# Strassen's seven half products for five projections of two column groups, in a hybrid SSM and pooling layer

## The chip, the cores and the metric

The kernel runs on one core of a Trainium2 chip. Its engines are PE (matrix products), DVE (vector operations), ACT (activations and copies), POOL (vector operations, and here the issue of some DMAs) and SP (issue of DMAs); each works through its own instructions in order, and semaphores tie them together. The metric is device microseconds of one launch; the median of three runs is given.

## What is computed

One inference step of a layer with two branches. 2064 prompt tokens (16 meta tokens ahead of 2048) and 8 x 8 sample tokens of 1024 features are normalised and projected six ways; an SSM branch and a causal pooling branch follow, each gated, and all is merged and added to the input. In float32:

```python
xn = rmsnorm(h, norm_gain)
proj = xn @ w_in                       # u_s, z_s, u_p, z_p and two gates, 1024 columns each
gates = jax.nn.sigmoid(proj[..., o4:] + b_gate)
y_s, new_re, new_im = ssm_branch(u_s, s0_re, s0_im, ...)   # scan, gelu, y * sigmoid(y @ w_glu + b_glu)
y_p, new_buf = pool_branch(u_p, buf, pos0, pool_mix, pool_scale)  # windows 2, 4, 8, 16, then a 256x256 mix each
a = y_s * jax.nn.silu(z_s)
b = y_p * jax.nn.silu(z_p)
merged = g_s * (a @ w_branch_ssm) + g_p * (b @ w_branch_pool)
return h + merged @ w_out, new_re, new_im, new_buf
```

The final norm and the new states are outputs as well.

## The kernel before

Features lie on the 128 partitions (eight blocks of 128), tokens along the free dimension, in four groups of columns (`GROUPS`): 544, 536, 536 and 512 wide. Group 3, the last one, holds the sample tokens too.

**Products.** Each operand is split into a high and a low part in the fp32r format, and a product is three matmuls: high by high, weight high by input low, weight low by input high (`mm3`, lines 126 to 128). `proj` makes one output block: eight input blocks, two halves of the columns in groups 0 to 2 (268 columns each in groups 1 and 2), one bank of 512 columns in group 3. That is one *unit*: 48 matmuls, or 24 in group 3. Its result lies in a PSUM tile `acc` of two banks; there are three such tiles, and a new unit takes the next one once the reader of its former contents is done.

**The list of units** is written out by hand for each stage: `up`, `zp` and `mix` of the pooling branch in the order of the string `ORDER`, then `gate` and `brp`, `zs`, `glu`, `gate` and `brs`, `out`. The main loop (line 1288 on) runs it. At unit i it issues the cast of the weights of unit i+2 to their high part (`w_high`, POOL), the posts of unit i-1 (what reads its PSUM: ACT or DVE, and what follows), events tied to the unit, the unit's matmuls with pieces of the SSM between them, then the weight low of unit i+2 (`w_low`, DVE, line 202) and loads of the weights of units i+3 to i+5 (`w_load`, SP, three buffers `raw`). A post therefore stands on its engine behind all that earlier units issued there.

**Pooling.** `up`'s post copies its block to `E` (ACT, line 797), POOL adds the two columns of history (line 800), DVE forms the running sums over 2, 4, 8 or 16 tokens (lines 813 to 823); `po_split` splits the result for `mix`, whose post (line 878) multiplies the gate in `H` by the mix in PSUM. One unit `mix` serves two blocks.

**The SSM** runs in two rounds of 32 pairs, 37 *ticks* each, spread over units of other work: round 0 over units 39 to 72, round 1 over units 76 to 212, none in the pooling stages (`spread`). Each tick issues small matmuls into the tiles `sx` and `sy`, DVE scans, ACT copies and POOL products; the result of a pair goes out from the one buffer `sY` by a DMA to `ys` (line 579).

```python
def st_out(g, q):
    y = stile("sY", 1, g.kn)
    A.activation(y, pr.pop(q)["py"], AF.Copy)
    SY.dma_start(chans(g, ys_d, q), y)
```

## Time and profile before

| | us |
|---|---|
| median of three runs | 2161.5 (2160.64 to 2164.21) |
| profiled run | 2158.2 |
| span of its trace | 2156.4 |
| busy PE, DVE, POOL, ACT | 2084.8, 1395.2, 931.2, 686.5 |

The trace is of one execution; its times count from the start of the span. The granted clock is TensorE's, 1.00 for its full speed, the mean of the span is 0.99. "DMA share" is the mean busy share of the core's 16 DMA engines. In a timeline a number in brackets is how long the engine stood idle before the instruction, and on whom it waited. Stages, in us: the SSM's first round to unit 72 ends at about 578; groups 2 and 3 begin their pooling stages at about 1284 and 1735.

### The profile page before, as it was taken

What the parts mean: (1) busy time and instruction counts of PE and PEld (TensorE: products, weight loads), DVE (VectorE), ACT (ScalarE), POOL (GpSimd) and SP (SyncE); (2) the same over time, 40 slices, a digit from 0 to 9 for tenths busy, and PEclk for the clock granted to TensorE, in tenths of its full rate; (3) what the DMA queues carried; (4) which work ended last, traced back from release to release, by engine and by line L of the source; (5) the groups of instructions that cost most, each with busy time, mean ns of one, the idle gap of its engine ahead of it and who ended that gap; (6) DMA issues with size and microseconds to landing.
All of it is one profiled execution on the core that took longest, in us unless ns stands there. A gap on an engine that the chain in (4) does not pass through costs nothing.

```text
span 2156.4 us, 37693 instructions
## 1 busy us (share of the span) xinstructions
PE 2084.8 (97%) x14968; PEld 1970.0 (91%) x14968; DVE 1395.2 (65%) x1916; ACT 686.5 (32%) x1243; POOL 931.2 (43%) x1054
## 2 busy tenths in 40 slices
PE   7999999889899999999999999999999999999998
PEld 7988899888799999999899999999999987888887
DVE  7889968978656686644856676634643767456444
ACT  3213357645444332144544332121210221112101
POOL 3387747655444452234644452233421333144222
PEclk9999999999999999999999999999999999999999
DMA  6646557586933543245444543234333433343233
GB/s 200 145 116 165 164 170 206 143 198 156 186 122 124 159 137 127 81 121 142 124 124 138 162 134 125 89 119 115 100 103 108 141 128 119 101 133 117 91 98 105
DMA packets 261279, 287.77 MB, mean 133 GB/s; under 512 B 106096, under 2 KB 203760, under 8 KB 261104
## 3 DMA queue, kind: packets, MB, share of 16 engines
q1 hardware_dynamic: 261104, 285.37, 45.8%
q8 instruction: 118, 1.93, 0.4%
q14 instruction: 57, 0.47, 0.1%
HBM read 242.32 MB, written 40.62 MB: 131 GB/s over the span
## 4 chain that ended last, share of the span: by engine, by line
PE 69%; DVE 7%; DMA 5%; ACT 3%; issue 2%; POOL 1%; SPq 0%; DVEq 0%; ACTq 0%; POOLq 0%
PE acc L126 22%; PE acc L128 22%; PE acc L127 22%; DMA ys<-sY 3%; DVE wl L202 1%; DVE sX L533 1%; DVE sph L554 1%; DVE sX L536 1%; PE sy L574 1%; PE sx L508 1%; DVE al L114 1%; PE sy L573 1%; DMA mat_d<-mp 1%; DVE sph L495 0%; ACT sXw L543 0%
## 5 line engine op out<-in xcount | busy, mean ns | idle before, releaser
L126 PE MATMUL acc<-ah,wh 128*128 128x268 f32 (+4 forms) x4504 | 1370.9, 304 | 8.9 <-ACT ah L698 6.6
L128 PE MATMUL acc<-ah,wl 128*128 128x268 f32 (+4 forms) x4504 | 1360.5, 302 | 4.8 <-DVE wl L202 4.8
L127 PE MATMUL acc<-al,wh 128*128 128x268 f32 (+4 forms) x4504 | 1359.0, 302 | 0.0
L126 PEld LDWEIGHTS acc<-ah,wh 128*128 128x128 f32 x4504 | 853.2, 189 | 43.2 <-issue 7.7
L128 PEld LDWEIGHTS acc<-ah,wl 128*128 128x128 f32 x4504 | 850.5, 189 | 33.1 <-DVE wl L202 5.9
L127 PEld LDWEIGHTS acc<-al,wh 128*128 128x128 f32 x4504 | 852.4, 189 | 27.5 <-issue 0.2
L103 POOL TENSOR_SCALAR wh<-raw 128x1024 fp32r<-128x1024 f32 (+1 forms) x336 | 395.9, 1178 | 964.2 <-PE acc L127 834.7
L202 DVE TENSOR_TENSOR wl<-raw,wh 128x1024 fp32r<-128x1024 f32 (+1 forms) x336 | 427.2, 1272 | 147.2 <-POOL wh L103 146.7
L890 ACT ACTIVATE sg<-acc,hb 128x536 f32<-128x536 f32 (+2 forms) x64 | 44.9, 702 | 404.0 <-PE acc L128 403.9
L524 DVE TENSOR_TENSOR sX<-sx,scc 128x270 f32<-128x270 f32 (+1 forms) x64 | 27.2, 424 | 106.5 <-ACT xs L518 66.3
L114 DVE TENSOR_TENSOR al<-H,ah 128x536 fp32r<-128x536 f32 (+3 forms) x96 | 88.4, 954 | 7.6 <-POOL ah L103 5.2
L946 DVE SCALAR_TENSOR_TENSOR H<-po,H 128x536 f32<-128x536 f32 (+2 forms) x32 | 25.4, 795 | 101.9 <-ACT po L944 101.9
L846 ACT ACTIVATE H<-acc 128x536 f32<-128x536 f32 (+2 forms) x64 | 39.0, 610 | 139.5 <-PE acc L128 139.1
L105 ACT ACTIVATE ah<-H 128x536 fp32r<-128x536 f32 (+3 forms) x80 | 50.7, 646 | 96.1 <-DVE H L878 77.4
L847 DVE SCALAR_TENSOR_TENSOR H<-H,acc 128x536 f32<-128x536 f32 (+2 forms) x64 | 44.8, 700 | 47.0 <-ACT H L846 46.5
L813 DVE TENSOR_TENSOR w<-E 128x483 f32<-128x483 f32 (+2 forms) x32 | 22.0, 687 | 74.2 <-POOL E L800 65.1
L573 PE MATMUL sy<-su,smc 128*128 128x135 f32 (+1 forms) x256 | 52.4, 286 | 18.1 <-ACT sY L578 15.1
L957 DVE SCALAR_TENSOR_TENSOR sg<-sg,acc 128x536 f32<-128x536 f32 (+2 forms) x32 | 22.4, 702 | 69.4 <-PE acc L128 69.4
L536 DVE TENSOR_TENSOR_SCAN sX<-r,state,sX 128x135 f32<-128x135 f32 (+1 forms) x128 | 65.6, 554 | 2.3
L944 ACT ACTIVATE po<-acc,hb 128x536 f32<-128x536 f32 (+2 forms) x32 | 22.5, 704 | 134.5 <-PE acc L128 134.5
L899 DVE SCALAR_TENSOR_TENSOR G<-sg,acc 128x536 f32<-128x536 f32 (+2 forms) x32 | 22.4, 700 | 64.2 <-PE acc L128 64.2
L574 PE MATMUL sy<-sS,smc 128*128 128x135 f32 (+1 forms) x256 | 53.4, 291 | 10.8 <-POOL sS L565 10.8
(232 smaller groups left out, 2271.0 us busy)
## 6 DMA issues: line engine op xcount, KB each, us to landing
raw<-in_wb SPq DMA_DIRECT2D x318, 512.0 KB, 3.8
smc<-mat_d SPq DMA_DIRECT2D x64, 256.0 KB, 4.1
smb<-mat_d SPq DMA_DIRECT2D x64, 128.0 KB, 3.2
xr<-in_xb SPq DMA_DIRECT2D x21, 268.0 KB, 4.3
H<-in_xb SPq DMA_DIRECT2D x19, 268.0 KB, 4.4
su<-us SPq DMA_DIRECT2D x32, 135.0 KB, 4.2
ys<-sY SPq DMA_DIRECT2D x32, 135.0 KB, 4.6
us<-po SPq DMA_DIRECT2D x16, 268.0 KB, 6.7
```

The costliest lines, as they stand in the source:

```text
L103: G.tensor_scalar(out, in_, 1.0, 0.0, ALU.mult, ALU.add)
L105: A.activation(out, in_, AF.Copy)
L114: V.tensor_tensor(l, x, h.bitcast(F32), ALU.subtract)
L126: PE.matmul(out, wh, xh, start=first, stop=False)
L127: PE.matmul(out, wh, xl, start=False, stop=False)
L128: PE.matmul(out, wl, xh, start=False, stop=last)
L202: V.tensor_tensor(l[:, c], r[:, c], h[:, c].bitcast(F32), ALU.subtract)
L536: V.tensor_tensor_scan(x[:, j], r8[:, i].to_broadcast([P, g.kp]), x[:, j], state[:, i], ALU.mult, ALU.add)
L573: PE.matmul(d["py"][:, j], d["m"][:, j, :P], d["u"][:, j], start=True, stop=False)
L574: PE.matmul(d["py"][:, j], d["m"][:, j, P:], d["S"][:, j], start=False, stop=True)
L847: V.scalar_tensor_tensor(self.v3(out), self.v3(out), 1.0, self.pv(ps), ALU.add, ALU.mult)
L890: A.activation(self.v3(s), self.pv(ps), AF.Tanh, scale=0.5, bias=hb[:, b, fb:fb + 1])
```

## The change

**Half products.** In groups 2 and 3 (`FAST`) the five projections of the normalised input (`up`, `zp`, `gp`, `zs`, `gs`) are made for a pair of output blocks at a time, with Strassen's scheme in Winograd's form: features are cut into two halves of four blocks, tokens into two halves (268 or 256 columns), output into its two blocks. Seven products of four input blocks each take the place of eight. A pair is four units, t0 to t3: two products in each of t0 to t2, one in t3. Their weights are tiles of 1024, 1024, 1024 and 512 columns. Sums of products are formed in PSUM (bank a gets four products in turn) and by subtractions on DVE and POOL from copies that ACT keeps in SBUF (`s_keep`).

**Sums of the weights** are made once, in DRAM: `w_sum` issues per pair one copy (SP) and three accumulating copies (POOL), of which each waits for the one before; 20 pairs, spread over units 60 to 145. **Sums of the inputs** are made in the output stage of the group before (`x_scale`, `s_op`), on POOL, DVE and ACT.

**Engines and order.** The casts of t1 and t3 go to ACT; the low of t1 goes to POOL for `up` and `zp`. The pooling stage's order is a new string, with pairs U, Z, G and the mixes m. Loads and gelu of `ys` move from the zs stage to the one before. Round 1 of the SSM now covers units 76 to 173 and ends with group 1; its memory is then closed (`end_ssm`) and used for the new tiles. In all groups `mm3` now takes both column halves in turn for each of its three products.

```diff
+FAST = (2, 3)
+HIGH_A = (1, 3)
+LOW_P = (W_UP, W_ZP)
+SUMS = 60
...
-        PE.matmul(out, wh, xh, start=first, stop=False)
-        PE.matmul(out, wh, xl, start=False, stop=False)
-        PE.matmul(out, wl, xh, start=False, stop=last)
+        for out, (xh, _) in zip(outs, xs):
+            PE.matmul(out, wh, xh, start=first, stop=False, skip_group_check=more)
+        for out, (_, xl) in zip(outs, xs):
+            PE.matmul(out, wh, xl, start=False, stop=False, skip_group_check=more)
+        for out, (xh, _) in zip(outs, xs):
+            PE.matmul(out, wl, xh, start=False, stop=last, skip_group_check=more)
...
+        eng = "a" if key[0] == "s" and key[1][2] in HIGH_A else "p"
         for c in cut(n, k):
-            cp("p", h[:, c], r[:, c])
+            cp(eng, h[:, c], r[:, c])
...
+        eng = G if key[0] == "s" and key[1][0] in LOW_P and key[1][2] == 1 else V
         for c in cut(n, k):
-            V.tensor_tensor(l[:, c], r[:, c], h[:, c].bitcast(F32), ALU.subtract)
+            eng.tensor_tensor(l[:, c], r[:, c], h[:, c].bitcast(F32), ALU.subtract)
+
+    def w_sum(base, p, step):
+        ws = ws_d[base][p]
+        q, dst = (((1, 0), ws), ((1, 1), ws[:, 0:3]), ((0, 0), ws[:, 1:4]), ((0, 1), ws[:, 2:3]))[step]
+        src = a["wb"][base + 2 * p + q[0]][:, 512 * q[1]:512 * (q[1] + 1)]
+        src = src.unsqueeze(1).to_broadcast(list(dst.shape))
+        if step:
+            G.dma_start(dst, src, accum_op=ALU.add)
+        else:
+            SY.dma_start(dst, src)
...
+        def s_unit(self, name, p, t, w):
+            if t == 0:
+                self.d = dict(zip("abc", self.s_banks()))
+                self.d["to"] = getattr(self, "to_" + name)(p)
+            d = self.d
+            a_, b_, c_, to = d["a"], d["b"], d["c"], d["to"]
+            if t == 0:
+                self.s_mm(a_, w, 0, "b11", True, 0)
+                self.s_keep("p1", a_)
+                self.s_mm(c_, w, 1, "t1", True, 0.5)
+                return lambda: self.s_keep("p5", c_)
+            if t == 1:
+                self.s_mm(a_, w, 0, "t2", False, 0)
+                self.s_keep("u2", a_)
+                self.s_mm(c_, w, 1, "b22", False, 0.5)
+                def post():
+                    for o, v in to(0, 1):
+                        V.tensor_tensor(o, v(c_), v(d["u2"]), ALU.subtract)
+                return post
+            if t == 2:
+                self.s_mm(a_, w, 0, "t3", False, 0)
+                self.s_keep("u3", a_)
+                self.s_mm(b_, w, 1, "b21", True, 0.5)
+                def post():
+                    for o, v in to(0, 0):
+                        V.tensor_tensor(o, v(b_), v(d["p1"]), ALU.subtract)
+                    for o, v in to(1, 1):
+                        G.tensor_tensor(o, v(d["u3"]), v(d["p5"]), ALU.subtract)
+                return post
+            self.s_mm(a_, w, 0, "t4", False, 0)
+            def post():
+                for o, v in to(1, 0):
+                    A.activation(o, v(a_), AF.Copy)
+                for j in range(2):
+                    getattr(self, "fin_" + name)(2 * p + j)
+            return post
...
+    def u_fast_pool(g):
+        for unit in "U0 Z0 U1 m0 Z1 U2 m1 Z2 U3 m2 Z3 G0 m3".split():
...
+    u_pool(g1)
+    busy = set(range(n, len(units)))
+    u_pgate(g1)
+    u_zs(g1, range(NB), True)
+    u_rest(g1, g2, 0)
+    spread(rounds[1], i + 2, len(units) - NB - 1, busy, BB)
+    for g, nxt in ((g2, g3), (g3, None)):
+        u_fast_pool(g)
         u_rest(g, nxt, 0)
-    at(hi, final_states)
+    todo = [(w, p) for w in W_FAST for p in range(NB // 2)]
+    for j, (w, p) in enumerate(todo):
+        for step in range(4):
+            at_part(SUMS + 4 * j + 3 * step, 0.5, w_sum, w, p, step)
```

**What moves, at three places.** In a row, `out<-in` names tiles with a running number, and brackets hold what the instruction waits for. The first place is DVE in the pooling stage of group 2, up to the two readers of a mix (`H<-acc,psc16,H`). Before:

```order
L114 TENSOR_TENSOR H3_15606<-po_15541,H2_15605 128x536 [waits Activation_49]
L202 TENSOR_TENSOR wl_15658<-raw_15464,wh_15598 128x1024 [waits DMAHW3_49,Pool_49]
L847 SCALAR_TENSOR_TENSOR H4_15664<-H4_15664,acc_15609 128x536 [waits Activation_49]
L202 TENSOR_TENSOR wl_15693<-raw_15524,wh_15662 128x1024 [waits DMAHW5_49,Pool_49]
L878 SCALAR_TENSOR_TENSOR H6_15468<-acc_15667,psc16_65,H6_15468 128x536 [waits PE_49]
L878 SCALAR_TENSOR_TENSOR H7_15600<-acc_15680,psc16_65,H7_15600 128x536 [waits DVE_49,PE_49]
```

After, at the mix behind pair U1:

```order
L1049 SCALAR_TENSOR_TENSOR po_15709<-w1_15705,E_15573 128x536 [waits DVE_49]
L1039 TENSOR_TENSOR w0_15713<-E_15574 128x483 [waits DVE_49,Activation_49,Pool_49]
L1040 TENSOR_TENSOR w0_15713<-E_15574 128x68
L1041 COPY w0_15713<-E_15574 128x1
L1039 TENSOR_TENSOR w1_15717<-w0_15713 128x414 [waits DVE_49]
L1040 TENSOR_TENSOR w1_15717<-w0_15713 128x2x68
L1041 COPY w1_15717<-w0_15713 128x2
L1049 SCALAR_TENSOR_TENSOR po_15721<-w1_15717,E_15574 128x536 [waits DVE_49]
L1233 SCALAR_TENSOR_TENSOR G5_11953<-G5_11953,sm_60,ss_14755 128x536
L1103 SCALAR_TENSOR_TENSOR H4_15431<-acc_15725,psc16_65,H4_15431 128x536 [waits PE_49]
L1103 SCALAR_TENSOR_TENSOR H5_15432<-acc_15738,psc16_65,H5_15432 128x536 [waits PE_49]
```

Before, the readers of a mix follow weight lows and the reader of a zp unit; now they follow the pooling of both blocks of the pair ahead (`E_15573` and `E_15574`; of the first only the last step is in the rows).

The second place is PE in the same stage, at the first unit that uses the PSUM tile which such a mix left. Before, the end of a mix and the unit behind it:

```order
L126 MATMUL acc_15680<-H2_15605,wh_15526 128x268
L127 MATMUL acc_15680<-H3_15606,wh_15526 128x268
L128 MATMUL acc_15680<-H2_15605,wl_15594 128x268
L126 MATMUL acc_15709<-ah_14529,wh_15598 128x268 [waits DVE_49,Pool_49]
L127 MATMUL acc_15709<-al_14530,wh_15598 128x268
L128 MATMUL acc_15709<-ah_14529,wl_15658 128x268
```

After, in the first unit of pair Z1, at the step from bank a (`acc_15768`) to bank c (`acc_15769`):

```order
L140 MATMUL acc_15768<-ah2_15053,wl_15692 128x268
L136 MATMUL acc_15768<-ah3_15129,wh_15676 128x268
L138 MATMUL acc_15768<-al3_15130,wh_15676 128x268
L140 MATMUL acc_15768<-ah3_15129,wl_15692 128x268
L136 MATMUL acc_15769<-ah0_14898,wh_15676 128x268 [waits DVE_49]
L138 MATMUL acc_15769<-al0_14899,wh_15676 128x268
L140 MATMUL acc_15769<-ah0_14898,wl_15692 128x268
```

Before, the unit behind the mix waits for DVE's reader of a unit ahead of the mix; now the second half of Z1's first unit waits for the mix's first reader on DVE, whose tile is `acc_15725` in the rows of DVE.

The third place is POOL around unit 63, in the SSM's first round. Before, weight casts (`wh<-raw`) and the products of a tick:

```order
L103 TENSOR_SCALAR wh_5881<-raw_5624 128x1024 [waits DMAHW5_49,PE_49]
L564 COPY sS_5914<-state_71 128x2 [waits PE_49]
L565 TENSOR_TENSOR sS_5914<-scc_5564,sph_5563 128x2x134 [waits DVE_49]
L566 TENSOR_TENSOR state_71<-scc_5564,sph_5563 128x2 [waits Pool_49]
L486 TENSOR_TENSOR sph_5918<-pA_67,pB_68 128x272 [waits Pool_49]
L489 TENSOR_SCALAR scc_5919<-sph_5918 128x272 [waits Pool_49]
L528 TENSOR_TENSOR sXw_5908<-sXw_5908,sph_5771 128x270 [waits DVE_49,Activation_49]
L103 TENSOR_SCALAR wh_5983<-raw_5733 128x1024 [waits DMAHW5_49,PE_49]
L103 TENSOR_SCALAR wh_6064<-raw_5879 128x1024 [waits DMAHW7_49,DVE_49,PE_49]
L103 TENSOR_SCALAR wh_6141<-raw_5981 128x1024 [waits DMAHW5_49,DVE_49,PE_49]
```

After:

```order
L609 TENSOR_TENSOR sS_5923<-scc_5572,sph_5571 128x2x134 [waits DVE_49]
L610 TENSOR_TENSOR state_86<-scc_5572,sph_5571 128x2 [waits Pool_49]
L530 TENSOR_TENSOR sph_5927<-pA_82,pB_83 128x272 [waits Pool_49]
L533 TENSOR_SCALAR scc_5928<-sph_5927 128x272 [waits Pool_49]
L572 TENSOR_TENSOR sXw_5917<-sXw_5917,sph_5780 128x270 [waits DVE_49,Activation_49]
L110 TENSOR_SCALAR wh_5992<-raw_5742 128x1024 [waits DMAHW6_49,PE_49]
L244 DMA ws16_99<-in_wb 128x3x512 [waits DMAHW3_49]
L110 TENSOR_SCALAR wh_6074<-raw_5888 128x1024 [waits DMAHW0_49,DVE_49,PE_49]
L110 TENSOR_SCALAR wh_6152<-raw_5990 128x1024 [waits DMAHW6_49,DVE_49,PE_49]
```

An accumulating copy (`ws16<-in_wb`) now stands between two weight casts, and waits for the landing of the copy that it adds to.

## Rows read from the trace of the kernel before

**Rows 1.** Busy time by stretch: us, each engine's busy us (instructions), granted clock, DMA share, GB/s.

```profile
468.00:578.00 110.00, 94.38 (x550) 82.48 (x550) 84.69 (x126) 55.24 (x114) 56.09 (x86) 0.97 0.83 176
578.00:1000.00 422.00, 415.97 (x3367) 414.90 (x3366) 263.18 (x369) 144.50 (x265) 176.07 (x213) 1.00 0.43 127
1284.00:1415.00 131.00, 131.00 (x1053) 130.85 (x1052) 80.70 (x134) 26.76 (x50) 34.44 (x44) 1.00 0.33 106
1415.00:1735.00 320.00, 320.00 (x2578) 319.37 (x2577) 153.26 (x173) 58.17 (x98) 105.81 (x101) 1.00 0.37 115
1735.00:1850.00 115.00, 114.50 (x495) 92.51 (x494) 78.47 (x137) 23.81 (x45) 36.22 (x55) 1.00 0.39 121
1850.00:2105.00 255.00, 255.00 (x1104) 206.81 (x1103) 123.36 (x130) 39.24 (x63) 83.43 (x74) 1.00 0.35 110
```

**Rows 2.** Waits of PE from 1284 to 2105 us: total us, times, longest.

```profile
PE acc L126 <- DVE H L878: 0.5, 1, 0.5
```

**Rows 3.** Chain of work that ended last, 468 to 578 us, shares by line.

```profile
by line: DMA ys<-sY 35.1%; issue 9.3%; PE acc L126 5.7%; PE acc L128 5.4%; PE acc L127 5.4%; DVE sX L533 4.0%; DVE wl L202 3.7%; DVE sX L536 3.7%; DVE sph L554 3.6%; ACT sXw L543 2.7%; DVE po L763 2.4%; ACT sXw L515 2.1%; ACT sXw L516 2.1%;
```

**Rows 4.** Timeline of ACT, zs units of groups 2 and 3: start, us, instruction [idle before].

```profile
1500.00 0.62 ACT L846 ACTIVATE H<-acc 128x536 f32<-128x536 f32 x1 [2.57 <-PE acc L128]
...
1541.81 0.62 ACT L846 ACTIVATE H<-acc 128x536 f32<-128x536 f32 x1 [3.29 <-PE acc L128]
...
1928.09 0.60 ACT L846 ACTIVATE H<-acc 128x512 f32<-128x512 f32 x1 [0.81 <-PE acc L128]
...
1966.97 0.60 ACT L846 ACTIVATE H<-acc 128x512 f32<-128x512 f32 x1 [2.91 <-PE acc L128]
```

**Rows 5.** Timeline of PE, tail, matmuls of 256 columns, first and last of 54.

```profile
2130.64 0.28 PE L126 MATMUL acc<-ah,wh 128*128 128x256 f32 x1
...
2136.89 0.28 PE L128 MATMUL acc<-ah,wl 128*128 128x256 f32 x1
```

**Rows 6.** Timeline of DVE, first step of one pooling and what follows its last.

```profile
1333.19 0.66 DVE L813 TENSOR_TENSOR w<-E 128x483 f32<-128x483 f32 x1 [0.94 <-ACT E L797]
...
1335.56 0.77 DVE L1004 SCALAR_TENSOR_TENSOR G<-G,sm,ss 128x536 f32<-128x536 f32 x1
...
1366.01 0.66 DVE L813 TENSOR_TENSOR w<-E 128x483 f32<-128x483 f32 x1 [3.63 <-ACT E L797]
...
1369.30 0.69 DVE L202 TENSOR_TENSOR wl<-raw,wh 128x512 fp32r<-128x512 f32 x1
...
1393.17 0.66 DVE L813 TENSOR_TENSOR w<-E 128x483 f32<-128x483 f32 x1 [1.64 <-POOL E L800]
...
1397.29 1.22 DVE L202 TENSOR_TENSOR wl<-raw,wh 128x1024 fp32r<-128x1024 f32 x1
...
1767.21 1.40 DVE L878 SCALAR_TENSOR_TENSOR H<-acc,psc,H 128x512 f32<-128x512 f32 x2
...
1832.19 0.76 DVE L813 TENSOR_TENSOR w<-E 128x574 f32<-128x574 f32 x1 [1.78 <-POOL E L800]
...
1836.73 0.66 DVE L827 SCALAR_TENSOR_TENSOR po<-w,E 128x64 f32<-128x64 f32 x1
```

**Rows 7.** Timeline of PE after a wait in the SSM's first round.

```profile
557.02 0.50 PE L573 MATMUL sy<-su,smc 128*128 128x135 f32 x2 [3.85 <-ACT sY L578]
...
558.99 0.79 PE L126 MATMUL acc<-ah,wh 128*128 128x512 f32 x1
...
561.69 0.39 PE L126 MATMUL acc<-ah,wh 128*128 128x512 f32 x1
```

**Rows 8.** DMA issues from 1284 to 1850 us: KB each, median us to landing.

```profile
raw<-in_wb SPq DMA_DIRECT2D x91, 512.0 KB, 3.7
```

**Rows 9.** Busy time by stretch, 600 to 640 us.

```profile
600.00:640.00 40.00, 40.00 (x330) 40.00 (x329) 23.34 (x25) 15.48 (x24) 19.09 (x18) 1.00 0.35 111
```

**Rows 10.** Timeline of SP's DMA issues.

```profile
548.28 0.67 SPq L916 DMA_DIRECT2D xr<-ys  x1
```

**Rows 11.** Groups of POOL instructions by shape, 1284 to 2105 us: busy us, mean ns.

```profile
L987 POOL TENSOR_TENSOR ss<-ss,po 128x536 f32<-128x536 f32 x9 | 16.4, 1823 | 5.5 <-ACT po L983 3.6 <-DVE H L752 1.8
```

More of the change, by code (lines that the diff above doesn't have):

```diff
@@ L673, in proj @@
                         x = [v[k][:, h * n:(h + 1) * n] for v in (xh, xl)]
-                    mm3(out, [x[:, k * P:(k + 1) * P] for x in w], x, k == 0, k == nk - 1)
+                    outs.append(out)
+                    xs.append(x)
+                mm3(outs, [x[:, k * P:(k + 1) * P] for x in w], xs, k == 0, k == nk - 1)
             return ps
@@ L680, in slot, with s_banks, s_mm @@
             return h, l
+        def s_banks(self):
+            odd, t = stage.get("odd"), psum.tile([P, 2, 512], F32, tag="acc", bufs=3, name="acc")
+            if odd is None:
+                c = psum.tile([P, 2, 512], F32, tag="acc", bufs=3, name="acc")
+                stage["odd"] = c
+                c = c[:, 0]
+            else:
+                stage["odd"], c = None, odd[:, 1]
+            return [x[:, :self.H2] for x in (t[:, 0], t[:, 1], c)]
+        def s_mm(self, out, w, j, x, first, pos):
+            xh, xl = self.op[x]
+            for k in range(4):
+                between(pos + k / 8)
+                mm3([out], [v[:, 512 * j + k * P:512 * j + (k + 1) * P] for v in w], [(xh[k], xl[k])],
+                    first and k == 0, k == 3, not first)
@@ new lines, in s_to, with to_zp, fin_silu, fin_zp @@
+        def s_to(self, tiles):
+            n = self.H2
+            return lambda j, h: [(tiles[j][:, h * n:(h + 1) * n], lambda x: x)]
+        def to_zp(self, p):
+            for f in (2 * p, 2 * p + 1):
+                self.sz[f] = self.t(tmp, f"H{4 + f % 4}")
+            return self.s_to([self.sz[2 * p], self.sz[2 * p + 1]])
+        def fin_silu(self, s, q):
+            A.activation(q, s, AF.Tanh, scale=0.5)
+            V.scalar_tensor_tensor(s, q, 1.0, s, ALU.add, ALU.mult)
+        def fin_zp(self, f):
+            self.fin_silu(self.sz[f], self.t(tmp, "sg", 3))
@@ L1109, in u_rest @@
             at(i + 1 + (f // 4 if ahead == 0 else 0), g.a_split, f)
-        for f in range(ahead, 3 if ahead else 2):
-            add("w", W_GS + f, g.gate, f, 0)
+        if g.fast:
+            u_fast(g, W_GS, "gs", 0)
+        else:
+            for f in range(ahead, 3 if ahead else 2):
+                add("w", W_GS + f, g.gate, f, 0)
         ahead = 3 if ahead else 2
@@ L1130, in u_rest @@
             at(i - 2, g.r_load, f, g.cols(h))
-            if nxt:
+            if nxt and nxt.fast:
+                if f == 0 and nxt is g2:
+                    at(i, final_states)
+                    at(i + 1, end_ssm)
+                for part in range(3):
+                    if 0 <= f - 2 - part < 4:
+                        at(i, nxt.s_op, f - 2 - part, part)
+            elif nxt:
                 if f == 0:
```

214 lines of the change are left out of this document (181 added, 33 removed).

## The prediction

> **What bounds the kernel now.** I read first the table by stretches [rows 1]: from 1284 to 2105 us, which is all of groups 2 and 3 but the two ends, PE is busy in 820.5 of 821 us. The list of waits agrees: PE waits there once, for 0.5 us [rows 2]. So in these two groups a matmul less is time less, provided that no other engine becomes late. DVE is the next one: 153 us of 320 in the projections of group 2, 78 of 115 in the pooling stage of group 3 [rows 1]. The stretch 468 to 578 us is of another kind: PE works 94 of 110 us, the DMA engines are 83% busy [rows 1], and in the chain of work 35.1% is the store of the SSM's result, ys<-sY [rows 3]. The change puts work into both kinds.
>
> **1. Matmuls removed.** A projection unit of group 2 is 48 matmuls of 268 columns. Between the first and the last of the eight zs units' first readers of PSUM lie 41.81 us, seven units [rows 4]: 5.97 us a unit and 124.4 ns a matmul. In group 3 it is 24 matmuls of 512 columns in 38.88/7 = 5.55 us, 231.4 ns each [rows 4]. Matmuls of 256 columns, which group 3 gets instead, occur in the tail of this trace: 53 steps in 6.25 us, 117.9 ns each [rows 5]. A pair of output blocks needs 84 half products of either width, against 96 (268 columns) or 48 (512 columns) before. Twenty pairs a group: group 2 -240 x 124.4 = -29.9 us; group 3 +1680 x 117.9 - 960 x 231.4 = 198.1 - 222.1 = -24.0 us. Together **-54 us**. Two 256-column matmuls cost 4.4 ns more than one of 512, so the ratio 7/8 is nearly kept. The new order inside mm3 I cost at nothing: matmuls in these units come at one pace, whether weights or bank change between two of them.
>
> **2. A mix right behind its U.** In the pooling stage PE's order becomes U, m, Z. The first half product into bank c of Z's first unit stands behind the mix's first reader on DVE (the PE rows of the change), and that reader stands on DVE behind the pooling of both blocks of U (the DVE rows), which is issued with what follows U's last unit. One pooling takes 2.37, 3.29 or 4.12 us for windows 4, 8 and 16 [rows 6]. Count from the end of U. DVE first ends a weight low (1.22 us, begun shortly before), at about 0.95 us; then come two poolings; then the mix's reader, 0.7 us [rows 6]. For windows 4, 8 and 16 it is done at 6.4, 8.2 and 9.9 us, and window 4 has one G step, 0.7 us [rows 6], in between: 7.1. PE needs the bank after the mix, 24 x 124.4 = 2.98 us, and half a unit, 1.49 us: at 4.5 us. It waits 2.6, 3.7 and 5.4 us, 12 us in group 2. In group 3 one pooling is 4.54 us to the start of its last step, some 4.8 with it, where group 2 has 4.12 [rows 6], 16% more, so 2.75, 3.8 and 4.8; PE is there at 12 x 231.4 + 12 x 117.9 ns = 4.2 us: waits of 2.9, 5.0 and 7.0 us, 15 us. **+27 us**. If DVE began the first pooling a microsecond earlier each time, 21; if the low and the splits behind the reader then make Z's later units late too, 40.
>
> **3. The clock behind long waits.** After a wait of 3.85 us at 557 us, six 512-column matmuls took 2.70 us [rows 7], 0.45 instead of 0.23 each: 1.3 us lost. Four or five of the six waits of step 2 are over 2.9 us: **+6 us**, 0 to 8.
>
> **4. Other waits in the fast units.** Four weight tiles a pair instead of two: per three units a raw buffer is loaded (3.7 us [rows 8]), cast and lowered (1.22 us on DVE [rows 6]), some 6.1 us with a cast like the low, and there are three units' 7.8 us for it, with three buffers. ACT's copy of bank a, under 0.62 us (its pass over twice the width [rows 4]), has the 1.49 us in which PE fills the other bank. I take **+2 us**, 0 to 15; the upper end is rival C's.
>
> **5. Weight sums beside the SSM's first round.** Sums are formed from unit 60 (about 468 us) on; up to unit 72 (578 us) these are four copies (1 MiB each) and six adds, 8.4 MB written. At the 111 GB/s that a share of 0.35 gave at 600 to 640 us [rows 9], full engines move 317 GB/s: 26 us of all engines. At this stretch's own 176 GB/s for 0.83 [rows 1] it is 40 us. Free are 0.17 x 110 = 19 us. So 8 to 21 us too much if an add costs as a copy does, 21 to 41 if it counts twice. The sums are pieces of 2 KB, so the first rate is nearer, 8. An issue from POOL doesn't occur in this trace; one from SP takes up to 0.67 us [rows 10], so six some 4 us, on an engine that is half idle: 2 for that. **+10 us**, 3 to 45: where the store of ys has slack less of it shows.
>
> **6. The other sums, 578 to about 1030 us.** In all 20 x 2.88 = 57.7 MB; less the 8.4, 49.3 MB or 155 us of all engines at 317 GB/s, against 0.57 x 422 = 240 us free up to 1000 us [rows 1]. It fits, with PE nearly full there. **+2 us**, 0 to 60.
>
> **7. The SSM's second round** gets a tick each 2.08 free units instead of 2.68, no tick less. Its long PE waits come with ticks, not with their distance; what is gained in group 2 is lost in group 1: **0**, -4 to +8. The operand sums (POOL, DVE, ACT) lie in the output stage of the group before, where PE is the bound: sixteen half-width two-input operations of POOL, some 0.9 us each by the 1.82 us of the full width [rows 11], 15 us in six units of 5.97; that cover is inside the range of step 4.
>
> **Sum**: -54 + 27 + 6 + 2 + 10 + 2 + 0 = -7 us. The profiled run of before took 2158.2 us (its span 2156.4), so 2151; the median of the three runs lies 3.3 us over the profiled one, so **2155 us** (2154.5). That is 0.3% faster; a measurement of this kernel can tell some 0.2%, or 4.3 us, from no change.
>
> **Rivals.**
> A. *The poolings and the sums don't reach PE.* If the first pooling starts before U's last unit ends, because its POOL step and its low come early, and the store of ys has slack, steps 2, 3 and 5 shrink to about 10, 2 and 3 us: -54 + 10 + 2 + 2 + 3 + 2 = -35, so 2126 us; if nothing at all waits, 2107. For it: DVE is only about half busy from 1415 to 1735 us [rows 1]. Against it: in that pooling stage (1284 to 1415) it is 62% busy already [rows 1], and what counts is its order.
>
> B. *The DMA engines run full* (the slower side). The accumulating copies don't occur in the trace of before. If one costs twice a copy, the rest of the sums is 155 us plus the adds' 32.5 MB at 317 GB/s, 103 us: 258 us against 240 free. From there on every load of weights is late, and POOL, which takes its casts and its adds in one order, stands at an add until the step before has landed (the POOL rows of the change); the casts queue behind it, and PE behind them. Price: 21 to 41 us in step 5 instead of 10, and some 18 us to 60 us in step 6: the sum is +20 to +82, so about 2182 to 2244 us, 2205 in the middle. It decides from the point at which an add takes more than 1.8 copies. For it: the share is 0.43 even without the sums [rows 1]. Against it: raw loads land in 3.7 us [rows 8] in far shorter time than the 24 us between two steps.
> The Trainium skill, "Collectives: The Full Stack", section "The bandwidth ceiling: the fold count and why AG ≠ RS ≠ AR", says that an add in a DMA needs two source reads and so runs at half the copy's rate. No run here shows it for a copy inside DRAM; by that rule alone B would hold and the time would be its 2205 us. The rows leave B short of room by 18 us only, so its chance stays at 0.22.
>
> C. *POOL is late with the low of the second tile* (up and zp, 128 x 1024, two inputs). A two-input operation of 536 columns takes 1.82 us on POOL [rows 11], so 1024 take 3.5 us; behind it stands the cast of the third tile, 1.1 us more, and DVE's low of it, 1.2: 5.8 us of the 5.97 until PE asks for it. If the start is a microsecond late, each of 16 pairs waits about a microsecond: +16, 2170 us.
> The Trainium skill, "GPSIMD Engine Reference", section "3.1 Elementwise — side-by-side cycle accounting", gives 4.5 us for 2048 elements with two inputs, so an estimate by that page is 2.25 us for 1024. The row says more, 1.82 us for 536, and the measurement decides; by the page C would not occur, and the sum would stay as it is.
>
> **How the numbers follow.** The sum of the steps, 2135 to 2175 us by itself, has a chance of 0.42 (faster 0.24, within 0.2% 0.10, slower 0.08); A 0.24, all faster; B 0.22, all slower; C 0.12 (slower 0.10, within 0.02). So faster 0.48, same 0.12, slower 0.40. The likeliest gives 2155. For 8 in 10 the range reaches into A down to 2118 and into B up to 2215; its lower end leaves out a gain without any wait, its upper end a long queue of sums.
>
> **What would show it.** In the profile after: (1) zs pairs of group 2 in 84 x 124.4 ns = 10.45 us, of group 3 in 9.9. (2) Three PE waits in each pooling stage for the mix's reader on DVE, 3 to 7 us long, the longest for window 16. (3) A granted clock under 1.00 behind them. (4) No weight wait in the zs and gs stages. (5) The stretch to unit 72 longer by some 10 us, with the share of ys<-sY in the chain as large as now or larger. (6) A DMA share of about 0.8 from 578 to 1030 us, PE still full. (7) No SSM tick after group 1. Wrong would be: waits of POOL on the adds' landing with PE idle behind (B), PE waiting for weights in the pooling stages (C), or a pooling stage without waits (A). If matmuls of 256 columns took over 125 ns in a long run, step 1 would lose 12 us and the sign would turn.

## The result: 7.4% slower, and the profile after

The changed kernel takes 2322.3 us (median of 4, 2317.3 to 2327.5) against 2162.4 us before, a ratio of 1.0739 (95% interval 1.0726 to 1.0752). The forecast was 2155 us with a range up to 2215: wrong in sign and far outside. The profiled run has a span of 2321.9 us, 165.5 more than before.

The table gives the stretches of both traces. A group ends with the last whole eviction of its output stage (the start of the last of DVE's L973 before, L1202 after).

| us | before | after | difference |
|---|---|---|---|
| start to the end of the SSM's first round (last `po` of `us`) | 581 | 604 | +23 |
| from there to the end of group 0 | 224 | 251 | +27 |
| group 1 | 481 | 484 | +3 |
| group 2 | 445 | 495 | +50 |
| group 3 and tail | 425 | 487 | +62 |

So the two groups that were to lose 54 us of matmuls gained 112. The stretches of the trace of after, to be read against [rows 1] (columns as there):

```profile
468.00:604.00 136.00, 110.19 (x601) 96.20 (x600) 90.10 (x127) 55.85 (x115) 68.50 (x95) 0.89 0.94 198
604.00:856.00 252.00, 234.34 (x1821) 231.23 (x1820) 173.71 (x216) 108.35 (x201) 148.54 (x180) 0.95 1.01 235
700.00:790.00 90.00, 89.97 (x731) 89.80 (x730) 60.38 (x82) 39.20 (x72) 52.13 (x72) 0.99 1.03 249
856.00:980.00 124.00, 122.43 (x986) 122.08 (x985) 80.81 (x133) 26.45 (x49) 49.55 (x57) 1.00 1.01 239
1345.00:1500.00 155.00, 122.64 (x855) 117.65 (x854) 112.03 (x161) 47.12 (x89) 60.71 (x54) 0.89 0.39 127
1586.00:1640.00 54.00, 47.55 (x355) 45.29 (x354) 42.06 (x40) 20.51 (x41) 29.20 (x19) 0.97 0.45 145
1840.00:1996.00 156.00, 118.13 (x798) 110.27 (x797) 115.10 (x177) 46.39 (x93) 65.53 (x72) 0.87 0.42 134
```

Before, PE was full in the pooling stages and in zs; now it is busy 123 of 155, 118 of 156 and 48 of 54 us. The granted clock fell to 0.89 and 0.87 in the pooling stages. From 604 to 980 us the DMA engines are full. That alone doesn't stop PE: from 700 to 790 us, beside ticks of the SSM, it is busy all the time, from 856 to 980, in group 1's pooling stage, 122 of 124 us. What is lost between 604 and 856 us lies at its two ends, 604 to 700 and 790 to 856, with 18 us of idle PE where the like stretches before have 6. The waits of PE from 1340 us to the end (total us, times, longest), where before there was one of 0.5 us [rows 2]:

```profile
PE acc L136 <- DVE H L1103: 44.4, 6, 9.6
PE acc L136 <- ACT u L755: 23.5, 40, 1.1
PE acc L136 <- DVE sg L785: 13.4, 16, 2.5
PE acc L954 <- POOL ss L1216: 12.4, 2, 6.2
PE acc L140 <- DVE wl L234: 11.5, 8, 2.9
PE acc L136 <- DVE E L785: 6.2, 10, 0.7
PE acc L136 <- DVE H L785: 5.1, 8, 0.9
PE acc L136 <- DVE xr L785: 4.1, 6, 1.2
```

The sums agree. Counted from the starts of the matmuls in the trace, what lies over 2.6 times the full-rate step is a wait, what lies between 1.5 and 2.6 times it is slow clock: 135 us of waits and 37 us of slow clock from 1340 us on, against 2 and 4 us in the same part before. -54 + 133 + 33 = +112, the table's 50 + 62.

Two of these waits need a closer look. First a pair of zs in PE's timeline, at the two steps into and out of bank b (start, us, instruction, idle before it):

```profile
1602.95 0.28 PE L140 MATMUL acc<-t43h,wl 128*128 128x268 f32 x1
1603.72 0.58 PE L136 MATMUL acc<-ah,wh 128*128 128x268 f32 x1 [0.48 <-ACT u L755]
...
1606.33 0.43 PE L140 MATMUL acc<-ah,wl 128*128 128x268 f32 x1
1607.36 0.40 PE L136 MATMUL acc<-t43h,wh 128*128 128x268 f32 x1 [0.60 <-DVE xr L785]
```

The second line is the first product into bank b. It waits for ACT's copy `u3` of bank a, which it doesn't touch; 0.77 us pass instead of 0.12. One product later, in the last line, the first matmul of t4 into bank a waits in the same way for DVE's reader of bank b (L785; 40 times, 28.8 us in the four rows with L785 above). Banks a and b are the two halves of one PSUM tile `acc`.

And DVE in the pooling stage, at the wait for window 16, with POOL at the same moment below it:

```profile
1458.34 0.30 DVE L1040 TENSOR_TENSOR w<-w 128x136 f32<-128x136 f32 x1
1458.56 2.35 DVE L1041 COPY w<-w 128x2 f32<-128x2 f32 x1
1460.95 1.25 DVE L1039 TENSOR_TENSOR w<-w 128x276 f32<-128x276 f32 x1
```

```profile
1458.45 2.44 POOL L234 TENSOR_TENSOR wl<-raw,wh 128x1024 fp32r<-128x1024 f32 x1
1460.86 1.04 POOL L110 TENSOR_SCALAR wh<-raw 128x1024 fp32r<-128x1024 f32 x1
```

A copy of two columns takes 2.35 us, and ends when POOL's subtraction with two inputs ends. The step behind it, of 276 columns, takes 1.25 us beside POOL's next instruction, a cast with one input; in the next block, with POOL idle, the same step takes 0.45. So a cast holds DVE as well. DVE's subtractions with one input in PSUM (L785, 268 columns) took 0.44 us whether they began beside a cast or not.

### The profile page after: what moved, and what is told of

Read it like the earlier page. It is cut to its first block, busy times and chain, and to the rows that moved or that the text cites. A ratio compares the mean times of both kernels' runs of the same rounds, so it can differ in the third digit from the quotient of the medians.

```text
span 2321.9 us, 39869 instructions
## 1 busy us (share of the span) xinstructions
PE 2105.2 (91%) x15448; PEld 2005.5 (86%) x15448; DVE 1585.8 (68%) x2084; ACT 816.3 (35%) x1514; POOL 1131.8 (49%) x1206
## 3 DMA queue, kind: packets, MB, share of 16 engines
q0 software_dynamic: 18880, 36.70, 10.5%
## 4 chain that ended last, share of the span: by engine, by line
PE 55%; DVE 13%; DMA 7%; issue 5%; ACT 4%; POOL 3%; SPq 1%; DVEq 0%; ACTq 0%; POOLq 0%
PE acc L136 18%; PE acc L138 17%; PE acc L140 17%; DMA ys<-sY 4%; DVE wl L234 3%; DVE al L121 1%; DMA xr<-ys 1%; DVE w L1039 1%; DMA smb<-mat_d 1%; POOL wh L110 1%; PE sx L552 1%; DVE w L1041 1%; PE sy L618 1%; DVE sX L577 1%; ACT u L755 1%
## 5 line engine op out<-in xcount | busy, mean ns | idle before, releaser
L136 PE MATMUL acc<-ah,wh 128*128 128x268 f32 (+4 forms) x4184 | 1000.9, 302 | 78.6 <-DVE H L1103 44.4
L140 PE MATMUL acc<-ah,wl 128*128 128x268 f32 (+4 forms) x4184 | 981.8, 297 | 9.3 <-DVE wl L234 9.0
L138 PE MATMUL acc<-al,wh 128*128 128x268 f32 (+4 forms) x4184 | 984.7, 298 | 0.5 <-DVE al L121 0.5
L136 PEld LDWEIGHTS acc<-ah,wh 128*128 128x128 f32 x4184 | 700.9, 193 | 111.3 <-DVE H L1103 45.6
L140 PEld LDWEIGHTS acc<-ah,wl 128*128 128x128 f32 x4184 | 698.6, 192 | 25.1 <-DVE wl L234 11.1
L138 PEld LDWEIGHTS acc<-al,wh 128*128 128x128 f32 x4184 | 700.7, 193 | 14.4 <-DVE al L121 0.9
L234 DVE TENSOR_TENSOR wl<-raw,wh 128x1024 fp32r<-128x1024 f32 (+1 forms) x400 | 519.4, 1302 | 84.2 <-POOL wh L110 69.1
L136 PE MATMUL acc<-t43h,wh 128*128 128x268 f32 (+1 forms) x320 | 97.6, 305 | 28.8 <-DVE sg L785 13.4
L140 PE MATMUL acc<-t43h,wl 128*128 128x268 f32 (+1 forms) x320 | 94.0, 294 | 11.5 <-DVE wl L234 11.5
L138 PE MATMUL acc<-t43l,wh 128*128 128x268 f32 (+1 forms) x320 | 93.2, 291 | 0.0
L617 PE MATMUL sy<-su,smc 128*128 128x135 f32 (+1 forms) x256 | 53.8, 292 | 26.9 <-ACT sY L622 15.3
L755 ACT ACTIVATE u<-acc 128x268 f32<-128x268 f32 (+1 forms) x80 | 31.0, 388 | 116.2 <-PE acc L140 115.5
```

Of the source, the lines that this page charges most:

```text
L136: PE.matmul(out, wh, xh, start=first, stop=False, skip_group_check=more)
L138: PE.matmul(out, wh, xl, start=False, stop=False, skip_group_check=more)
L140: PE.matmul(out, wl, xh, start=False, stop=last, skip_group_check=more)
L234: eng.tensor_tensor(l[:, c], r[:, c], h[:, c].bitcast(F32), ALU.subtract)
L617: PE.matmul(d["py"][:, j], d["m"][:, j, :P], d["u"][:, j], start=True, stop=False)
L755: A.activation(t, bank, AF.Copy)
```

## The experiments

All kernels are the changed kernel with the edits shown. Where totals differ by less than 15 us the stretches are compared, for a reason that the first run shows.

**The changed kernel again.**

```diff
+AGAIN = True
```

> The changed kernel once more (a constant is added that nothing reads), beside the others on one chip, to see how much of a difference between runs lies in the stretch up to the end of group 0, where the sums share the DMA engines with the SSM: that stretch took 855 us in its first profile and 859 to 869 us in four kernels that are the same up to there. All theories expect groups 2 and 3 to take 495 and 487 us as in the first profile, within 2 us; if the first stretch takes 860 us or more, totals of single kernels differ by 10 us for no edit, and only the times of stretches can be compared.

2329.0 us; 860 us up to the end of group 0, then 483, 495 and 488. Groups 2 and 3 repeat within 1 us. The first stretch doesn't: over the kernels that are the same up to there it took 855 to 869 us. It is the stretch in which the sums run.

**Bank b in a tile of its own.**

```diff
-            return [x[:, :self.H2] for x in (t[:, 0], t[:, 1], c)]
+            b = sw["pb"].tile([P, 512], F32, tag="b", bufs=2, name="accb")
+            return [x[:, :self.H2] for x in (t[:, 0], b, c)]
```

> The changed kernel with bank b in a PSUM tile of its own (two buffers of one bank, in the space that the SSM's tiles leave), nothing else. In the trace of the changed kernel PE stands once per pair before the first product into b (0.48 us behind ACT's copy of bank a) and once before the last product into a (0.60 us behind DVE's reader of bank b), about 0.65 and 0.8 us with the restart. Theory 1 (the waits come only from a and b being two banks of one tile): both are gone, 40 pairs x some 1.45 us = 58 us less, part of the slow clock goes too, 2250 to 2270 us. Rival (ACT and DVE really are needed there, or are late for other reasons): the waits move to the next matmul and the time stays at 2315 to 2330 us.

2287.6 us, with a first stretch of 866: groups 2 and 3 took 468 and 464 us, 50 less. The waits for L755's `u` and for L785 left the list; of what is left from 1353 us on, the first rows are

```profile
PE acc L136 <- DVE H L1104: 50.7, 6, 10.5
PE acc L140 <- DVE wl L234: 18.7, 10, 3.9
PE acc L955 <- POOL ss L1217: 12.4, 2, 6.2
PE acc L136 <- ACT p L756: 8.1, 6, 3.0
```

Theory 1 is shown: the 80 waits came from the two banks being one tile to the program's semaphores. (The edit also gives the pair two more banks of PSUM; a run with more banks alone wasn't made, but the reader waited for was each time one of the same pair's other bank.) Some 20 us of the waits came back, as longer ones for the mix's reader, weights and ACT's `p`.

**Each mix behind a Z.**

```diff
-        for unit in "U0 Z0 U1 m0 Z1 U2 m1 Z2 U3 m2 Z3 G0 m3".split():
+        for unit in "U0 Z0 U1 Z1 m0 U2 Z2 m1 U3 Z3 m2 G0 m3".split():
```

> The changed kernel with the units of the pooling stage in another order, each mix behind a Z instead of behind a U (U0 Z0 U1 Z1 m0 U2 Z2 m1 U3 Z3 m2 G0 m3). Theory 2 (the mix's reader on DVE stands behind two poolings, and that alone makes the six long waits, 44.4 us in the changed kernel): the waits for the mix's reader fall under 5 us, the granted clock of the two pooling stages rises from 0.89 and 0.87 to over 0.95, and the time falls by 45 to 65 us to 2257 to 2277 us. Rival (DVE is too full in these stages whatever the order): the waits come back in another place and the time falls by less than 15 us.

2341.8 us: no gain, groups 2 and 3 at 498 and 491. The waits for the mix's reader fell from 44.4 to 8.3 us, but from 1350 us on the list is now headed by

```profile
PE acc L140 <- DVE wl L234: 43.9, 14, 7.9
```

Theory 2 fell in its second half: what stands on DVE behind a U delays whatever is next, the mix's reader or the weight lows.

**The first pooling a unit earlier.**

```diff
+                    if name == "up":
+                        self.fin_up(2 * p)
                 return post
...
-                for j in range(2):
+                for j in range(1 if name == "up" else 0, 2):
```

> The changed kernel with the pooling of a pair's first block issued behind the third of its four units, where its data are complete, instead of behind the fourth. Theory 2a (the mix's reader is late because two poolings stand ahead of it in one piece): the first pooling starts some 1.5 us earlier and runs beside U's last unit, the six long waits shrink by 1 to 2.5 us each, 2307 to 2317 us. Rival (DVE is behind at this place already, so that an earlier place in its order changes nothing): 2319 us or more.

2324.4 us, groups 2 and 3 at 490 and 488. The same exchange: 10.8 us of waits for the mix's reader, and 34.3 us for lows from 1344 us on (11.5 in the changed kernel). By itself the earlier place is worth 4 us in the two groups.

**The low of the second tile on DVE.**

```diff
-LOW_P = (W_UP, W_ZP)
+LOW_P = ()
```

> The changed kernel with the low of the second weight tile back on DVE for up and zp, so that POOL has no operation of 1024 columns with two inputs. In the trace of the changed kernel that operation takes 2.42 us, and DVE's instructions that run beside it are drawn out (a copy of 2 columns 2.35 us where others take 0.16, a subtraction of 536 columns 2.49 where others take 0.72). Theory 4 (POOL's two-input operation keeps DVE from reading): the drawn-out instructions are gone, DVE's busy time in the pooling stage falls from 112 us though eight lows of 1.2 us are added, the long waits for the mix's reader fall by 1 to 3 us each, 2295 to 2312 us. Rival (DVE is short of time there, not held up): DVE's busy time rises by 10 us, the waits grow, 2322 us or more.

2320.5 us, but with a first stretch of 869; groups 2 and 3 took 486 and 481 us, 14 less. The groups of DVE's instructions in the pooling stage of group 2 (count, busy us, mean ns), first of the changed kernel, then of this one:

```profile
L121 DVE TENSOR_TENSOR H<-po,H 128x536 fp32r<-128x536 f32 x8 | 12.4, 1547 | 3.3 <-ACT H L112 3.3
L1041 DVE COPY w<-w 128x2 f32<-128x2 f32 x6 | 7.5, 1258 | 0.0
```

```profile
L121 DVE TENSOR_TENSOR H<-po,H 128x536 fp32r<-128x536 f32 x8 | 7.1, 893 | 3.4 <-ACT H L112 3.4
L1041 DVE COPY w<-w 128x2 f32<-128x2 f32 x6 | 0.9, 158 | 0.0
```

Theory 4 is shown for the drawn-out instructions: without POOL's operation the copy takes 158 ns instead of 1258. DVE's busy time stayed at 112 us, since it has the lows now; the six long waits fell from 44.4 to 37.9 us. The size expected of the total wasn't reached, or can't be seen behind the first stretch.

**Shorter poolings.**

```diff
-            for step in range(wi + 1):
+            for step in range(1 if self.fast else wi + 1):
```

> The changed kernel with the pooling of groups 2 and 3 cut to its first step in all blocks (so windows 4, 8 and 16 are computed as window 2; the pooled outputs of these groups are not the reference's). DVE is relieved of some 12 us per pooling stage. Theory 2b (DVE has more to do in the pooling stage than PE's time there, so whatever its order is, PE waits for it): the long waits nearly vanish, the clock comes back, each pooling stage falls by 20 to 32 us from 158, 2265 to 2285 us. Rival (the poolings are a small part, weights are late by themselves): each falls by less than 12 us, the DVE time taken away, and PE still waits over 25 us there.

2305.5 us; both pooling stages (from the end of the group before to the last mix's reader) took 146 us, 12 less than the 158 of the changed kernel, about the DVE time taken away (10 and 12 us by its busy time). Waits of 21.8 us for the mix's reader remain, up to 4.4 each, and 28 and 32 us of all kinds in the two stages. Theory 2b fell: DVE is busy 112 of 158 us there before the edit and 102 of 146 after it, so it isn't short of time over the whole stage. That each stage fell by about the time taken away says that the poolings stand on the path where they are. What the waits left are made of was not shown; POOL's subtraction is part of it, since a step of 0.66 us still takes 2.80 beside it (at 1396.14 us).

**Three edits together** (own bank, low on DVE, earlier pooling).

> The changed kernel with three edits together: bank b in a tile of its own, the second tile's low on DVE, the first pooling issued a unit earlier. If the causes add (35 us measured for the bank, 10 to 25 for the low, 5 to 15 for the pooling), 2245 to 2275 us. If DVE is the bound of the pooling stages once the bank waits are gone, the three do not add: 2275 us or more, with the long waits for the mix's reader as before.

2267.2 us; groups 2 and 3 at 459 and 457. The stretches fell by 36 and 30 us, 66 in all, where the three alone took 50, 14 and 4 off the two groups: they add. The waits for the mix's reader went down to 19.7 us, 3.9 at most; 32.2 us from 1350 us on are waits for weights.

**No weight sums.**

```diff
-                SY.dma_start(r[:, 512:], ws[:, 0])
+                SY.dma_start(r[:, 512:], a2[:, :512])
...
-            at_part(SUMS + 4 * j + 3 * step, 0.5, w_sum, w, p, step)
```

> The changed kernel without the weight sums: no copy and no accumulating copy is issued, and where a unit would load a sum it loads plain weights of the same size, so the output of the five projections of groups 2 and 3 is not the reference's. Theory 3 (the sums fill the DMA engines from 470 to 1090 us and delay the SSM's stores and the weights): the stretch up to the end of group 0 gets 45 to 55 us shorter, time 2265 to 2280 us, and groups 2 and 3 stay as they are. Rival (the loss there comes from the SSM's second round being denser or from the new matmul order): less than 15 us, 2307 us or more.

2279.8 us: 817 us up to the end of group 0 (38 less than in the first profile, 43 less than in the repeat), groups 1 to 3 at 480, 494 and 486. Theory 3 is shown for the sums as a whole, a little under the 45 to 55 us expected. 12 us over before remain in the first stretch. Part of this is work moved, not lost: 48 instead of 32 of the 128 matmuls L617 of the SSM's second round stand ahead of that end, and none is left in group 2, where 16 were.

**Copies instead of adds.**

```diff
-            G.dma_start(dst, src, accum_op=ALU.add)
+            G.dma_start(dst, src)
```

> The changed kernel with each accumulating copy made a plain copy of the same bytes (issued by POOL at the same places), so the summed weights, and with them the five projections of groups 2 and 3, are not the reference's. Theory 3a (an add costs the DMA engines twice a copy): the software queue's share falls from 10.5% of the span to about 5%, the stretch from 604 to 856 us is no longer at a DMA share of 1.0, and 15 to 35 of the 50 us lost up to the end of group 0 come back. Rival (it is the bytes, or POOL's 1.2 us per issue and its waits, not the adding): less than 8 us come back.

2300.2 us, first stretch 839, 16 to 21 less than with adds: about half of the loss. The DMA queue rows (packets, MB, share of 16 engines), of the changed kernel and of this one:

```profile
q0 software_dynamic: 18880, 36.70, 10.5%
```

```profile
q0 software_dynamic: 9920, 36.70, 6.1%
```

The same bytes take 244 us of all engines as adds and 140 as copies, a factor of 1.7 and nearly twice the packets. Theory 3a's numbers were met. But POOL's time for an issue fell as well, from 1.15 to 0.74 us on average, so this run doesn't separate the engines' time from POOL's.

**Sums later.**

```diff
-            at_part(SUMS + 4 * j + 3 * step, 0.5, w_sum, w, p, step)
+            at_part(SUMS + 5 * j + 4 * step, 0.5, w_sum, w, p, step)
```

(and `SUMS = 76`)

> The changed kernel with the weight sums begun at unit 76 instead of 60 and spread to unit 183, the end of group 1, instead of 145 (a pair every five units, its steps four units apart). Theory 3 (the sums' loss comes from DMA engines that are full already in the SSM's first round, and full at 1.01 from 604 to 980 us): the stretch from 441 to 604 us falls back by some 20 us, half of the 27 us up to the end of group 0 come back, group 1 loses a few: 2285 to 2300 us. Rival (the work of the sums costs the same wherever it lies, by POOL's issues or by the SSM's stores): 2310 us or more.

2294.7 us: 584 us up to the end of the first round (604), 820 up to the end of group 0, and 496 in group 1, 12 more. The sums are cheaper begun later and spread thinner, not free; which of the two helps wasn't separated.

**Four edits together** (the three, and the later sums).

> Four edits together: bank b in a tile of its own, the second tile's low on DVE, the first pooling a unit earlier, and the weight sums from unit 76 to 183. The first three gave 459 and 457 us for groups 2 and 3 (495 and 487 in the changed kernel), the last alone 820 us for the stretch up to the end of group 0 and 496 for group 1. If they add: 820 + 496 + 459 + 457 = 2232 us span, 2228 to 2240 us. If sums that reach into the end of group 1 delay group 2's weights, more than 2245 us.

2231.4 us (1.0301 of before, 1.0270 to 1.0332), 822 + 494 + 457 + 458 us: they add, to 1 us in the span. No version tried within this scheme is faster by more than the spread of its runs, and it is still slower than the kernel before. Its groups 2 and 3 hold 78 us of waits and 28 of slow clock by the count above, the first for weights (29.0 us, 18 times) and the mix's reader (22.0 us, 6 times).

**The sum of squares.** POOL's subtractions for the input sums on DVE, on top of the four:

```diff
-                G.tensor_tensor(y2, x2, y2, ALU.subtract)
+                V.tensor_tensor(y2, x2, y2, ALU.subtract)
```

(and the three like it)

> The four edits and, besides, the subtractions that make the input sums on DVE instead of POOL (16 of half width in the output stages of groups 1 and 2). In the changed kernel PE waits 6.2 us at the end of each of these stages for POOL's sum of squares, and POOL is busy without a pause there. Theory 5 (POOL is overfull in these output stages): both waits fall under 2 us, 8 to 14 us less than the four edits alone. Rival (DVE takes over the part of the late engine, or the last sum of squares waits for ACT): less than 4 us.

2240.1 us, 9 more than the four. The two waits stayed:

```profile
PE acc L957 <- POOL ss L1219: 11.2, 2, 5.8
```

Theory 5 fell. Then the norm two units later:

```diff
-            at(i + 2, g.norm)
+            at(i + (4 if nxt.fast else 2), g.norm)
```

> The four edits and, besides, the norm of the group that is done and the steps behind it two units later. With POOL's subtractions moved to DVE PE's wait for the last sum of squares stayed at 5.8 us, so POOL's load is not its cause. Theory 5a (the norm's matmul is tied to the second unit after the output stage, and these units are now half as long, 2.98 us, so PE reaches it before the chain of eviction, square and sum is through): the waits for the sum of squares, 5.6 to 6.1 us at the ends of groups 1 and 2, fall under 1 us and the time by 8 to 14 us, 2217 to 2224 us. Rival (the chain itself is late by queueing and would be late at any place): under 4 us less.

2235.8 us (2229.9 and 2241.7; the profile is of the slower one). The waits for the sum of squares are gone, so it was the place, as theory 5a says: an event tied to the second unit after a stage comes half as late when units are half as long. But the time didn't fall. In the pooling stage of group 2, waits for ACT's `p` (L756) rose from 2.6 to 7.1 us, in that of group 3 from 8.1 to 15.1, and the stages took 145 and 156 us against 141 and 149. That the gain was taken back at this next place fits, but with 12 us between two runs of one kernel the profile of the slower one doesn't show it.

**The other order on top.** The edit of the mix's place again, on the kernel with the later norm:

> The four edits, the later norm, and each mix behind a Z instead of a U. With the order alone the waits moved from the mix's reader to weight lows and the time rose by 10 to 19 us, when two poolings, drawn out by POOL, stood on DVE in one piece. Theory 2c (once the first pooling is issued earlier and POOL no longer holds DVE, what stands on DVE behind U is short enough for the other order to gain): waits for the mix's reader nearly gone, weight waits not above 15 us in the two pooling stages, each stage 6 to 12 us shorter than in the same kernel with the mix behind U. Rival (DVE's work behind a U delays the lows of the units behind it as long as before): each stage no shorter, or longer, weight waits above 25 us.

2235.3 us; the pooling stages took 141 and 149 us, 4 and 7 less than with the mix behind U, and no less than in the four edits. But this profile is of the faster of two runs (2230.4 and 2240.2), the one before of the slower, and the medians are alike, so no gain is shown. Weight waits in the two stages are 21.7 us, between the two theories' numbers. What is shown is that the order no longer costs the 10 to 19 us that it cost alone.

## Why the prediction was wrong, step by step

**Step 1 held.** In group 2 the matmuls of 268 columns start every 123.6 ns, in group 3 those of 256 every 118.4 ns, where no wait or slow clock lies between. The 54 us were saved on PE and then waited away.

**Step 2 named the mechanism and mis-sized it.** The six waits are there, longest for window 16: 5.3, 6.7 and 8.2 us in group 2, 6.6, 7.9 and 9.6 in group 3, 44.4 in all against the 27 of the sum. Each is 2.6 to 3.7 us over its term. The term that was missing is POOL, which stops DVE in the middle of the first pooling: at window 16 of group 2 the copy lost 2.2 us to the subtraction and the step behind it 0.8 to the cast, 3.0 together, and the wait lies 2.8 over its term. With the lows back on DVE the six waits fell by only 1.1 each; my estimate is 1.0, the copy's 2.2 less the low of 1.2 that DVE then does itself, and the casts stay. Rival C had POOL's subtraction in view, but only as late by itself. The kernel before shows the same at a small scale, in a row that the prediction leant on: the last step at 1836.73 us took 0.66 us [rows 6], which I passed over as an oddity. POOL's cast ran beside it from 1836.23 to 1837.29 us; the seven other steps of this form took 0.24 at the median.
The Trainium skill, "GPSIMD Engine Reference", section "1. Specifications", says that POOL's interfaces to SBUF are shared with VectorE, with contention against VectorE's instructions that are in a 2-port perf mode or have two SBUF inputs. The traces agree for two SBUF inputs: DVE's step of 276 columns took 1.25 us beside a cast and 0.45 without, and L785, with one input in PSUM, 0.44 either way. For the copy the runs show 158 ns against 1258, but not its mode. The same page of the Trainium skill, section "3.1 Elementwise — side-by-side cycle accounting", gave 2.25 us as an estimate for POOL's operation; it took 2.42, where my scaling from 536 columns [rows 11] said 3.5: the page was near and the scaling wrong.

**Step 3 was sized too small by a factor of five.** 33 us more of slow clock in groups 2 and 3, not 6. Behind the wait of 8.17 us, which ended at 1468.98, the granted clock was 0.50, the lower of its two levels, to 1474 us:

```profile
1469.00:1474.00 5.00, 5.00 (x22) 5.00 (x23) 3.85 (x5) 2.46 (x5) 0.00 (x0) 0.50 0.14 28
```

21 steps of 268 columns took 4.69 us there, 223 ns each instead of 123.6: 2.1 us lost, where I took 1.3 from one place in the SSM [rows 7]. And there were some hundred waits of all kinds, not five long ones; the granted clock fell to 0.50 in some dozen stretches.

**Step 4 is the one that failed outright.** It set 2 us for all other waits in the fast units, because ACT's copy of bank a had half a unit of time. It didn't look at which semaphore the next product waits for. The first product into bank b waits for the reader of bank a, and the first of t4 for the reader of b, 80 waits of 52 us and 50 us of the time. Both waits are part of the program: each of the 40 pairs has them, and a and b are halves of one tile in `s_banks`, so they could have been read before any run, as the step from a to c was. The trace of before couldn't show it, since there a tile of two banks was filled and read as one.

**Steps 5 and 6 were at 12 us, and cost 42 to 49** (2322.3 or 2329.0 against 2279.8 without sums). What I took as rival B is what happened: a DMA share of 1.01 at 235 GB/s from 604 to 856 us, raw loads landing in a median of 9.0 us there (3.8 in the same stretch before), the stores of ys in 10.5 (3.4). In the first round (468 to 604 us) PE waited for loads of the SSM's matrices,

```profile
PE sy L617 <- DMA smc<-mat_d: 7.3, 2, 4.6
PE sx L552 <- DMA smb<-mat_d: 4.7, 2, 2.4
```

where before it did so once, for 1.1 us; for POOL it waited only 1.9 us there. Between 604 and 856 us its waits are for weight lows (4.5 us) and these matrices (4.9 us) first. B's clause that POOL stands at an add until the step before has landed did not come true: POOL waited 3.1 us for sums in all. I took POOL's issue as one of SP's, up to 0.67 us [rows 10]; it took 1.2:

```profile
L244 POOL DMA_DIRECT2D ws<-in_wb x27 | 31.5, 1165 | 0.3
```

The Trainium skill, "Collectives: The Full Stack", section "The bandwidth ceiling: the fold count and why AG ≠ RS ≠ AR", puts the collective whose add needs two source reads at half the rate of the one that copies. Here an add took 1.7 of a copy's engine time: close to the rule, and just below the 1.8 at which B was to decide. It was enough because the rate was wrong too. I took 317 GB/s for full engines; they moved 235 at a share of 1.01, and with plain copies 250 at 0.88 (604 to 839 us), which I scale to an estimate of 284. With 284 and the measured 1.74, step 6 and B's adds come to some 258 us against the 240 free.

**Step 7** was right in sum for group 1 (+3 us); the 16 matmuls L617 that left group 2 went to the stretch ahead of group 1, not into it. Its clause on the output stage wasn't: 12.4 us of waits for the sum of squares, whose cause is an event tied to units that are now half as long.

**Rivals.** A and the forecast's own range are refuted. B's price for the sums, 39 to 101 us in steps 5 and 6, holds the 42 to 49 that they cost; its time, 2182 to 2244, was passed, since even B left out the bank waits. C did not occur as told: POOL wasn't late, it made DVE late.

Added up, the misses are 17 us in step 2, 27 in step 3, 62 in step 4 (the bank waits and 11.5 us for weight lows, less its 2), 30 to 37 in steps 5 and 6 and 12 in step 7: some 150 of the 167 us between forecast and result.

What stays open: the 106 us of waits and slow clock that groups 2 and 3 keep after four edits. They were traced to weights and the mix's reader, not taken apart further; the order alone and the earlier pooling alone moved them from one to the other. Open too is how much of the sums' cost is the engines' and how much POOL's time for the issues.

## What to carry to other kernels

Before costing a step at "hidden", read in the new order which semaphore the next instruction of the full engine waits for; buffers that are read and written at different times need tiles of their own, even if they are different banks. A full engine that gets its work cut into shorter pieces also gets every look-ahead, counted in pieces, cut short: weights, norms and posts then come late one after another, and waits bring slow clock behind them (33 us to 133 us of waits here). A saving of matmuls that adds traffic should be priced against the DMA engines' free share with adds at 1.7 copies, and a helper on POOL, with one input or two, against DVE's time as well as its own.

## What the runs showed of the hardware

While POOL ran a subtraction of 1024 columns with two SBUF inputs (2.42 us), DVE's copies of two columns and its subtractions with two SBUF inputs that came up waited for its end (2.35 us for a copy of 0.16). POOL's casts, with one input, held DVE's two-input operations in the same way (1.25 us for a step of 0.45), and DVE's subtractions with one input in PSUM weren't held (0.44 us). An accumulating copy in DRAM took 1.7 times the DMA engine time of a plain one; an issue from POOL took 1.15 us of POOL as an add and 0.74 as a plain copy. Full DMA engines didn't stop PE by themselves: at shares of 1.01 and 1.03 it was busy 212 of 214 us (700 to 790 and 856 to 980 us). Behind a wait of 8.17 us the granted clock was 0.50 for 5 us, and matmuls of 268 columns came every 223 ns instead of 123.6.
